# A second 7-product block in every other pair of MLP chunks, with splits in one piece

## The chip, the cores and the metric

The kernel runs on one core of one Trainium2 chip. The metric is the device time of one execution in microseconds. The kernel before takes 2026.78 us, the median of three runs (2024.16 to 2027.75). Five engines run their own queues of instructions in order: TensorE (PE in the profile; its weight loads are shown apart as PEld), VectorE (DVE), ScalarE (ACT), GpSimd (POOL) and SyncE (SP). The last two mostly issue transfers here.

## What is computed

Two layers of a decoder work on x, 256 tokens by 2048 values in float32. The first layer mixes tokens by latent attention and a pooling mixer, the second by a gated short convolution. Each is followed by the part that the change touches:

```
h = rmsnorm(x, mlp_norm_g[layer])
x = x + square(relu(h @ w_up)) @ w_down     # w_up 2048 x 8192, w_down 8192 x 2048
```

The result has float32 accuracy, which the kernel reaches by splitting: every matrix is taken as a high and a low part in the format fp32r, and a product is three matmuls, high by high, high by low, low by high.

## The kernel before

**Splitting the weights.** Weights come as slabs of 1 MB (128 partitions by four blocks of 512 columns) into one of three buffers, tag "raw", loaded through SyncE's queue. `halved` splits a slab in two pieces of 128x1024: ScalarE casts a piece to the high part (line 141), VectorE subtracts to get the low part (line 142). There are six buffers for high and six for low pieces, used in turn; a piece's cast cannot start before TensorE has done its last matmul on the piece six before.

**The MLP.** `mlp` takes the 8192 hidden columns in 16 chunks of 512, two by two: eight pairs. `up_chunk` multiplies h by four slabs of w_up (lines 161 and 162, through `columns_steps`, 16 pairs of matmuls a slab), adds the two halves of the sum (line 195 a copy by ScalarE, line 197 a sum by VectorE), takes relu (732) and square (734), splits the hidden values into hT (201, 202) and forms four differences of them (746 to 748), which are split into fT. The down product of a pair of chunks runs in the time of the next pair's up chunks.

**The 7-product form.** For the first seven pairs, columns 0 and 1 of the down product (two blocks of 512 of the 2048 columns) are made by `down_seven`: seen as 2 by 2 blocks on tokens and hidden rows, the product needs seven block products in place of eight (the form of Strassen and Winograd). A product is 12 matmuls of 512 columns (lines 772 to 774). Its right sides are weight blocks b11, b12, b21, b22 and sums of them. The sums are made by transfers that add into the buffers t and v in memory on chip, issued by GpSimd (line 766), four for each pair. Three products go straight onto x (`onto`, line 801, a VectorE instruction that scales by r2, the reciprocal mean square of each token, and adds); four go into the totals p1, p5, p6, p7 (line 794), which are combined onto x in the seventh pair. Columns 2 and 3 are made by `down_block`, 96 matmuls for both (lines 154 to 156), with sums onto x at line 864. The last pair has four such plain blocks and no up chunks beside it.

**What sets the order.** The program text gives only a list of steps: generators of the up chunks, the products and the plain blocks are advanced in an order written out in the loop over p. A scheduler then places every instruction in its engine's queue by when it takes it to be ready, so the order in a queue is not the order of the text. Once built, each queue is fixed: an instruction that waits holds up all behind it on its engine. On VectorE the splits, the sums of products and the work on hidden values share one queue.

Of the kernel before, what the change touches and what calls it, by code (L numbers as in the profile page):

```python
# [16 lines left out]
P = 128  # L17
# [50 lines left out]
def trunk(ctx: ExitStack, tc, x_in, pos_in, mix_g, mlp_g, w_up, w_down, w_in, qa_g, kva_g, w_uq, w_ukv,  # L68
# [8 lines left out]
    def new_stage(raw_bufs=0, **more):  # L77
# [11 lines left out]
    small = ctx.enter_context(tc.tile_pool(name="small", bufs=2))  # L89
    acts = ctx.enter_context(tc.tile_pool(name="acts", bufs=4))  # L90
# [32 lines left out]
    def slab(src, kt, cols, sub=2, dmas=1, pieces=None):  # L123
# [8 lines left out]
    def halved(raw, sub=2, pieces=None):  # L132

        kt, cols = raw.shape[1], raw.shape[2]
        out_ = []
# [42 lines left out]
    def columns_steps(pss, w, xT, c0, n):  # L178
# [3 lines left out]
        for s in range(KD // rows_):  # L182
            ws = slab(w[s * rows_ * P:(s + 1) * rows_ * P, c0:c0 + n * P], rows_, n * P, sub=rows_ // 2)
# [8 lines left out]
    def sum_halves(ps, name):  # L192

        t = small.tile([P, 2, S], F32, tag="t", name=uid("t"))
        nc.scalar.copy(t, ps[:, :, S:2 * S])  # L195
        u = small.tile([P, 2, S], F32, tag="u", name=uid(name))
        nc.vector.tensor_tensor(out=u, in0=ps[:, :, 0:S], in1=t, op=ALU.add)
        return u
# [15 lines left out]
    new_stage(3)  # L214
# [71 lines left out]
    def squares(ss, b):  # L286

        for t in range(T):
            junk = small.tile([P, NB], F32, tag="t", name=uid("junk"))
# [22 lines left out]
    def over_tokens(r, pool):  # L312

        ps = bank2()
        for t in range(T):
            rb = small.tile([P, P], F32, tag="rb", name=uid("rb"))
# [54 lines left out]
    def latents():  # L371
# [12 lines left out]
        for t in range(T):  # L384
            for i in range(2):
                junk = small.tile([P, NB], F32, tag="t", name=uid("junk"))
# [77 lines left out]
    for g in reversed(range(GROUPS)):  # L464
        ps = bank2()
        for s in range(2):
            c0 = LAT + g * 2 * P
            ws = slab(w_in[0, s * 8 * P:(s + 1) * 8 * P, c0:c0 + 2 * P], 8, 2 * P, sub=4)
# [20 lines left out]
        m = small.tile([P, 2, S], F32, tag="u", name=uid("pm"))  # L489
# [6 lines left out]
    def rotate(src, t, heads, tables):  # L496

        own, other = (a[:, t, :].unsqueeze(1).to_broadcast([P, heads, ROPE]) for a in tables)
        turned = small.tile([P, heads, ROPE], F32, tag="t", name=uid("turned"))
# [5 lines left out]
    def square_sum(out_, a):  # L505
        n = a.shape[1]
        junk = small.tile([P, NB], F32, tag="t", name=uid("junk"))
# [69 lines left out]
    ws = slab(pool_w[0].rearrange("g c d -> (g c) d"), 2 * GROUPS, 2 * P, sub=4)  # L577
# [134 lines left out]
    def mlp(layer, ss, xT, after=None):  # L712
        up, down = w_up[layer], w_down[layer]
        hid, sums, totals = {}, {}, {}
# [4 lines left out]
        def up_chunk(c):  # L719

            pss = []
            yield from columns_steps(pss, up, xT, c * NB, 4)
            hT = act_tile()
            seven = c < 2 * (pairs - 1)
            if seven:
                fT = pools["forms"].tile([P, 2, 2, 4, P], F32R, tag="fT", name=uid("fT"))
            hid[c] = hT
            if seven:
                sums[c] = fT
            for i, ps in enumerate(pss):  # L730
                u = sum_halves(ps, "h")
                nc.scalar.activation(u, u, AF.Relu)
                sq = small.tile([P, 2, S], F32, tag="sq", name=uid("sq"))
                nc.scalar.activation(sq, u, AF.Square)
                split(hT[:, 2 * i:2 * i + 2, 0:S], hT[:, 2 * i:2 * i + 2, S:2 * S], sq)
                if seven:
                    sum_forms(fT[:, i], sq.rearrange("p e (t s) -> p (e t) s", t=T))
# [5 lines left out]
        def sum_forms(fT, a):  # L743

            f = small.tile([P, 4, P], F32, tag="u", name=uid("f"))
# [5 lines left out]
        def down_seven(pair):  # L751
# [3 lines left out]
            rows_ = down[2 * pair * NB:2 * (pair + 1) * NB].rearrange("(q e p) n -> e p q n", e=2, p=P)  # L755

            def at(e, n):
                return rows_[e][:, :, n * NB:(n + 1) * NB]
# [9 lines left out]
            def product(o, b, left):  # L768

                for q, (hi, lo) in enumerate(halved(b)):  # L770
# [3 lines left out]
                    nc.tensor.matmul(o, lhsT=a_lo, rhs=hi, start=False, stop=q == 3)  # L774

# [9 lines left out]
            def summed(name, o):  # L785

                if pair == 0:
                    totals[name] = pools["forms"].tile([P, NB], F32, tag=name, name=uid(name), bufs=1)
                    nc.scalar.copy(totals[name], o)
                else:  # L790
                    plus(totals[name], totals[name], o)

            def plus(out_, a, b):
                nc.vector.tensor_tensor(out=out_, in0=a, in1=b, op=ALU.add)

            def minus(out_, a, b):
                nc.vector.tensor_tensor(out=out_, in0=a, in1=b, op=ALU.subtract)

            def onto(t, n, part):
                xb = x[:, t, n * NB:(n + 1) * NB]  # L800
                nc.vector.scalar_tensor_tensor(out=xb, in0=part, scalar=r2[0][:, t:t + 1], in1=xb, op0=ALU.mult, op1=ALU.add)

            yield
            b11 = block(0, 0)
            t = block(0, 1, "t")
            add(t, 0, 0)
            one = bank2()
            product(one[:, 0, :], b11, own(0, 0))
            summed("p1", one[:, 0, :])
            yield  # L810
            v = block(0, 1, "v")
            add(v, 1, 1)
            product(one[:, 1, :], t, form(1))
            add(t, 1, 1)
            summed("p5", one[:, 1, :])
            yield
            two = bank2()
# [164 lines left out]
```

## Time and profile before

| | before |
|---|---|
| runs, median of 3 | 2026.78 us (2024.16 to 2027.75) |
| the profiled execution | 2025.33 us |
| its span | 2023.5 us |
| TensorE busy | 2005.9 us, 99%, 10534 matmuls |
| VectorE busy | 1389.5 us, 69%, 1739 instructions |
| ScalarE busy | 1120.1 us, 55%, 1480 instructions |
| GpSimd busy | 124.4 us, 6% |
| read from memory | 453.79 MB, 225 GB/s over the span |

The span is the time between the first and the last instruction of the profiled execution; its own time has 1.8 us around it. "Busy" counts an instruction from its start to its end; on TensorE and VectorE one starts before the last has ended, so durations add to more than the time they take together. In rows of a timeline the first number is the start, the second the duration, and in brackets stands the idle time before, with what ended it. In a table by windows the second number is the window's length, and behind the five engines' busy times (with counts) come the granted clock of TensorE (1.00 is full speed), the share of the 16 DMA engines that was busy, and GB/s. Rows of grouped instructions give their count, busy time and mean duration (ns), and end with the idle time just before them and what ended it.

### The profile page before, as it was taken

Reading aid. Unit: us, or ns where it says so; the run is one execution under the profiler, and the core shown is the slowest. Engines: PE = TensorE matmul, PEld = TensorE weight load, DVE = VectorE, ACT = ScalarE, POOL = GpSimd, SP = SyncE. Lnnn points to the kernel's source line nnn. Section 1 sums busy time; section 2 is a strip of 40 time slices with the busy share of each in tenths; the row PEclk is TensorE's granted clock in tenths of the full one; section 3 lists DMA queues with packets and bytes.
Section 4 is the critical chain, followed back from the end, with each engine's and each line's share of the span. In section 5 each row is a group of like instructions: output and inputs, shape, how many; then the busy total and the mean of one; then the engine's idle time right before and its main releaser. Section 6 shows DMA issues by size and latency. Waiting matters only on the chain.

```text
span 2023.5 us, 26714 instructions
## 1 busy us (share of the span) xinstructions
PE 2005.9 (99%) x10534; PEld 1722.5 (85%) x10534; DVE 1389.5 (69%) x1739; ACT 1120.1 (55%) x1480; POOL 124.4 (6%) x132
## 2 busy tenths in 40 slices
PE   8999999999999999999999999999999999999999
PEld 7987888888888888888888888888888888888887
DVE  5767567677766777776666656567777777777774
ACT  5457456565555655555444444456555566555552
POOL 2240000000000000000000000000000000000000
PEclk9999999999999999999999999999999999999999
DMA  7555577998989889865555557758898988989773
GB/s 245 161 173 177 182 219 215 270 247 242 281 252 264 245 258 257 263 208 187 179 190 188 190 191 226 231 177 222 267 255 265 270 239 265 257 253 270 217 224 125
DMA packets 232782, 457.62 MB, mean 226 GB/s; under 512 B 7344, under 2 KB 17456, under 8 KB 232656
## 3 DMA queue, kind: packets, MB, share of 16 engines
q1 hardware_dynamic: 202704, 396.91, 58.5%
q0 software_dynamic: 29920, 59.00, 17.1%
q8 instruction: 82, 1.34, 0.3%
q14 instruction: 44, 0.36, 0.0%
q10 hardware_dynamic: 32, 0.01, 0.0%
HBM read 453.79 MB, written 2.10 MB: 225 GB/s over the span
## 4 chain that ended last, share of the span: by engine, by line
PE 98%; DMA 1%; ACT 1%; SPq 0%; issue 0%; DVE 0%; ACTq 0%
PE ps L161 32%; PE ps L162 16%; PE ps L154 11%; PE ps L155 11%; PE ps L156 11%; PE ps L772 4%; PE ps L774 4%; PE ps L773 4%; PE ps L167 1%; PE ps L168 1%; PE ps L169 1%; PE ps L298 1%; DMA raw<-in_even_w_in 1%; PE ps L615 0%; ACT hi L141 0%; PE ps L619 0%
## 5 line engine op out<-in xcount | busy, mean ns | idle before, releaser
L142 DVE TENSOR_TENSOR lo<-raw,hi 128x1024 fp32r<-128x1024 f32 (+2 forms) x694 | 847.8, 1227 | 413.9 <-ACT hi L141 409.6
L141 ACT CAST hi<-raw 128x1024 fp32r<-128x1024 f32 (+2 forms) x694 | 724.8, 1049 | 620.9 <-PE ps L161 285.2
L161 PE MATMUL ps<-xT,hi 128*128 128x512 f32 x2816 | 988.9, 394 | 0.0
L162 PE MATMUL ps<-xT,lo 128*128 128x256 f32 x2816 | 789.5, 280 | 0.0
L161 PEld LDWEIGHTS ps<-xT,hi 128*128 128x128 f32 x2816 | 529.5, 188 | 122.1
L162 PEld LDWEIGHTS ps<-xT,lo 128*128 128x128 f32 x2816 | 527.6, 187 | 3.7
L154 PE MATMUL ps<-hi,hT 128*128 128x512 f32 (+1 forms) x896 | 349.1, 390 | 0.0
L156 PE MATMUL ps<-hi,hT 128*128 128x512 f32 (+1 forms) x896 | 347.3, 388 | 0.0
L155 PE MATMUL ps<-lo,hT 128*128 128x512 f32 (+1 forms) x896 | 347.2, 388 | 0.0
L154 PEld LDWEIGHTS ps<-hi,hT 128*128 128x128 f32 x896 | 168.3, 188 | 35.1 <-issue 1.3
L156 PEld LDWEIGHTS ps<-hi,hT 128*128 128x128 f32 x896 | 168.2, 188 | 34.7
L155 PEld LDWEIGHTS ps<-lo,hT 128*128 128x128 f32 x896 | 168.3, 188 | 33.6 <-DVE lo L142 0.4
L142 DVE TENSOR_TENSOR lo<-t,hi 128x1024 fp32r<-128x1024 f32 x84 | 102.6, 1221 | 45.2 <-ACT hi L141 45.1
L141 ACT CAST hi<-t 128x1024 fp32r<-128x1024 f32 x84 | 87.3, 1051 | 73.2 <-PE ps L161 50.7
L766 POOL DMA_DIRECT2D t<-in_w_mlp_down x42 | 54.4, 1296 | 1107.0 <-DVE lo L142 720.3
L772 PE MATMUL ps<-hi,fT 128*128 128x512 f32 x224 | 88.1, 393 | 0.0
L774 PE MATMUL ps<-hi,fT 128*128 128x512 f32 x224 | 87.7, 391 | 0.0
L773 PE MATMUL ps<-lo,fT 128*128 128x512 f32 x224 | 87.1, 389 | 0.0
L195 ACT COPY t<-ps 128x512 f32<-128x512 f32 x88 | 50.9, 579 | 40.6 <-PE ps L162 40.4
L772 PE MATMUL ps<-hi,hT 128*128 128x512 f32 x168 | 65.8, 392 | 0.0
L774 PE MATMUL ps<-hi,hT 128*128 128x512 f32 x168 | 65.6, 391 | 0.0
L773 PE MATMUL ps<-lo,hT 128*128 128x512 f32 x168 | 65.4, 389 | 0.0
(186 smaller groups left out, 1582.3 us busy)
## 6 DMA issues: line engine op xcount, KB each, us to landing
raw<-in_w_mlp_up SPq DMA_DIRECT2D x128, 1024.0 KB, 7.2
raw<-in_w_mlp_down SPq DMA_DIRECT2D x114, 1024.0 KB, 6.4
raw<-in_odd_w_in SPq DMA_DIRECT2D x48, 1024.0 KB, 5.1
t<-in_w_mlp_down POOLq DMA_DIRECT2D x42, 1024.0 KB, 13.5
raw<-in_even_w_out SPq DMA_DIRECT2D x16, 1024.0 KB, 5.4
raw<-in_odd_w_out SPq DMA_DIRECT2D x16, 1024.0 KB, 5.3
t<-in_w_mlp_down SPq DMA_DIRECT2D x14, 1024.0 KB, 5.8
v<-in_w_mlp_down SPq DMA_DIRECT2D x14, 1024.0 KB, 5.8
```

The costliest lines, as they stand in the source:

```text
L141: a = nc.scalar.copy(h, r)
L142: v = nc.vector.tensor_tensor(out=l, in0=r, in1=h.bitcast(F32), op=ALU.subtract)
L154: nc.tensor.matmul(o, lhsT=a_hi, rhs=hi[:, c0:c0 + n], start=first, stop=False)
L155: nc.tensor.matmul(o, lhsT=a_hi, rhs=lo[:, c0:c0 + n], start=False, stop=False)
L156: nc.tensor.matmul(o, lhsT=a_lo, rhs=hi[:, c0:c0 + n], start=False, stop=last)
L161: nc.tensor.matmul(o, lhsT=hi[:, c0:c0 + P], rhs=act[:, kt, :], start=first, stop=False)
L162: nc.tensor.matmul(o[:, S:2 * S], lhsT=lo[:, c0:c0 + P], rhs=act[:, kt, 0:S], start=False, stop=last)
L195: nc.scalar.copy(t, ps[:, :, S:2 * S])
L766: nc.gpsimd.dma_start(b, at(e, n), accum_op=ALU.add)
L772: nc.tensor.matmul(o, lhsT=a_hi, rhs=hi, start=q == 0, stop=False)
L773: nc.tensor.matmul(o, lhsT=a_hi, rhs=lo, start=False, stop=False)
L774: nc.tensor.matmul(o, lhsT=a_lo, rhs=hi, start=False, stop=q == 3)
```

## The change

Three things are changed.

First, a slab is split in one piece of 128x2048, with three buffers for high and three for low parts of that size (the same memory as six of half the size). The first stage alone, with the attention's latent columns, keeps six, in which some slabs are smaller.

Second, in the first, third, fifth and seventh pair (p even, "double") columns 2 and 3 take the 7-product form as well. Its steps are named with a prime, one' to four'. Here the sums of weight blocks are made by VectorE (`combine`, four of 128x2048 each), not by transfers, and the products go straight onto x, with r2 or its negative, except two that go into one total "w", which is combined onto x in the seventh pair. Such a pair loads ten weight blocks for the down product where it loaded nine (five and four). The forms of chunk A are made at the end of the chunk. The second, fourth and sixth pair keep the plain blocks.

Third, the order of steps is written as a list of names, and small buffers share one tag of four. Lines move: the split is 143 and 144 in the changed kernel (141 and 142 before), the up matmuls 163 and 164 (161, 162), a product 783 to 785 (772 to 774), sums into totals and weight blocks 798 (794), sums onto x 810 (801).

```diff
-    def slab(src, kt, cols, sub=2, dmas=1, pieces=None):
+    def slab(src, kt, cols, sub=None, dmas=1, pieces=None):
...
+        sub = sub or kt
...
-        for wanted in (dict(raws=raw_bufs, halves=6) if raw_bufs else {}, more):
+        for wanted in (dict(raws=raw_bufs, halves=half_bufs) if raw_bufs else {}, more):
...
     def sum_halves(ps, name):
 
-        t = small.tile([P, 2, S], F32, tag="t", name=uid("t"))
-        nc.scalar.copy(t, ps[:, :, S:2 * S])
-        u = small.tile([P, 2, S], F32, tag="u", name=uid(name))
-        nc.vector.tensor_tensor(out=u, in0=ps[:, :, 0:S], in1=t, op=ALU.add)
+        u = small.tile([P, 2, S], F32, name=uid(name), **T4)
+        nc.scalar.copy(u, ps[:, :, S:2 * S])
+        nc.vector.tensor_tensor(out=u, in0=ps[:, :, 0:S], in1=u, op=ALU.add)
         return u
...
+            def combine(out_, a, b, op):
+                nc.vector.tensor_tensor(out=out_, in0=a, in1=b, op=op)
+
+            def onto(t, n, part, r=0):
+                xb = x[:, t, (n0 + n) * NB:(n0 + n + 1) * NB]
+                nc.vector.scalar_tensor_tensor(out=xb, in0=part, scalar=r2[r][:, t:t + 1], in1=xb, op0=ALU.mult, op1=ALU.add)
...
+            def one():
+                b11 = block(0, 0)
+                w["v"] = block(0, 1, "v")
+                p = product(b11, own(0, 0))
+                combine(w["v"], w["v"], b11, ALU.add)
+                onto(0, 0, p)
+                summed("w", p)
+
+            def five():
+                p = product(w["v"], form(1))
+                onto(0, 1, p)
+                onto(1, 1, p)
+
+            def three():
+                w["t"] = block(0, 1, "t")
+                b22 = block(1, 1)
+                p = product(b22, form(3))
+                combine(w["t"], w["t"], b22, ALU.add)
+                combine(w["v"], w["v"], b22, ALU.add)
+                onto(0, 1, p)
+
+            def seven():
+                p = product(w["t"], form(0))
+                onto(1, 1, p)
+                onto(1, 0, p, 1)
+
+            def six():
+                summed("w", product(w["v"], form(2)), ALU.subtract)
+
+            def two():
+                b21 = block(1, 0)
+                p = product(b21, own(0, 1))
+                combine(w["v"], w["v"], b21, ALU.add)
+                onto(0, 0, p)
+
+            def four():
+                onto(1, 0, product(w["v"], own(1, 1)))
+                if final:
+                    onto(0, 1, totals["w"], 1)
+                    onto(1, 0, totals["w"])
+                    onto(1, 1, totals["w"], 1)
...
+        ONE_SEVEN = ("one A five A three A seven A six n A A n A two B four B B B m B B m B", "A one A five three A seven A six n A A n A two B four B B B m B B m B")
+        TWO_SEVENS = "one A five A three A seven A six one' A A two B five' B four B three' seven' six' A B two' B B four' B"
         for p in range(pairs - 1):
-            products = down_seven(p)
...
+            double = p % 2 == 0
+            steps = dict(A=up_chunk(2 * p + 2, double), B=up_chunk(2 * p + 3), n=down_block(p, 2, False), m=down_block(p, 3, False))
+            products = down_seven(p, 0, False)
+            if double:
+                products.update((k + "'", f) for k, f in down_seven(p, 2, True).items())
+            for step in (TWO_SEVENS if double else ONE_SEVEN[p > 0]).split():
+                if step in products:
+                    products.pop(step)()
+                else:
+                    next(steps[step], None)
```

In the order's rows a name's number tells its buffers apart; "hi" and "lo" are the parts of a slab, "raw", "t" and "v" weight blocks, "ps" a product on TensorE's side, "h" a chunk's hidden values.

The middle of the third pair of the first layer, on VectorE, before: splits of the buffer t for "six" (lo799, lo801), of the block for "two" (lo805, lo807) and of an up slab (lo820, lo822), in halves.

```order
L142 TENSOR_TENSOR lo799_4826<-t754_4559,hi798_4825 128x1024
L142 TENSOR_TENSOR lo801_4830<-t754_4559,hi800_4829 128x1024
L142 TENSOR_TENSOR lo805_4851<-raw803_4848,hi804_4850 128x1024
L794 TENSOR_TENSOR p7544_3357<-p7544_3357,ps777_4695 128x512
L142 TENSOR_TENSOR lo807_4855<-raw803_4848,hi806_4854 128x1024
L142 TENSOR_TENSOR lo820_4917<-raw818_4914,hi819_4916 128x1024
L197 TENSOR_TENSOR h811_4886<-ps760_4584,t810_4884 128x512
L142 TENSOR_TENSOR lo822_4921<-raw818_4914,hi821_4920 128x1024
```

The same place now; the up slab is lo628, "six" is lo612, one' is lo617, and "two" is lo623:

```order
L144 TENSOR_TENSOR lo612_4473<-t584_4239,hi611_4472 128x2048
L144 TENSOR_TENSOR lo617_4496<-raw613_4490,hi616_4495 128x2048
L198 TENSOR_TENSOR h619_4515<-ps587_4259,h619_4515 128x512
L144 TENSOR_TENSOR lo623_4532<-raw621_4529,hi622_4531 128x2048
L798 TENSOR_TENSOR p6450_3221<-p6450_3221,ps605_4416 128x512
L198 TENSOR_TENSOR h620_4522<-ps588_4260,h620_4522 128x512
L144 TENSOR_TENSOR lo628_4553<-raw626_4550,hi627_4552 128x2048
```

Between the splits of the block for "two" and of the up slab stand a sum into p6 and a sum of hidden values. On TensorE, at that place now, the last matmuls on the up slab before "two", and the first of "two" (hi622 and lo623):

```order
L164 MATMUL ps625_4549<-xT326_2237,lo628_4553 128x256
L163 MATMUL ps624_4548<-xT326_2237,hi627_4552 128x512
L164 MATMUL ps624_4548<-xT326_2237,lo628_4553 128x256
L163 MATMUL ps624_4548<-xT326_2237,hi627_4552 128x512
L783 MATMUL ps615_4494<-hi622_4531,hT541_3895 128x512
L784 MATMUL ps615_4494<-lo623_4532,hT541_3895 128x512
```

Eleven matmuls of the up slab stand before "two", and the other 21 behind it.

The end of the same pair on VectorE, before: lo837 and lo839 are splits of t for "four", ps797 is "two", ps835 is "four".

```order
L142 TENSOR_TENSOR lo837_5019<-t754_4559,hi836_5018 128x1024
L864 SCALAR_TENSOR_TENSOR x_79<-ps802_4847,r2468_2923,x_79 128x512 x2
L142 TENSOR_TENSOR lo839_5023<-t754_4559,hi838_5022 128x1024
L142 TENSOR_TENSOR lo842_5042<-raw840_5039,hi841_5041 128x1024
L801 SCALAR_TENSOR_TENSOR x_79<-ps797_4824,r2468_2923,x_79 128x512
L142 TENSOR_TENSOR lo844_5046<-raw840_5039,hi843_5045 128x1024
```

The same place now: ps647 is two', lo667 the split of v for four', ps665 four', lo672 the next up slab. On TensorE two', four' and that slab follow one another.

```order
L810 SCALAR_TENSOR_TENSOR x_79<-ps647_4742,r2392_2775,x_79 128x512
L144 TENSOR_TENSOR lo667_4861<-v614_4492,hi666_4860 128x2048
L203 TENSOR_TENSOR fT650_4760<-f652_4767,fT650_4760 128x512
L203 TENSOR_TENSOR hT659_4831<-h660_4832,hT659_4831 128x2x256
L751 TENSOR_TENSOR f662_4840<-h660_4832 128x256
L203 TENSOR_TENSOR hT659_4831<-h663_4846,hT659_4831 128x2x256
L752 TENSOR_TENSOR f662_4840<-h660_4832,f662_4840 128x128
L753 TENSOR_TENSOR f662_4840<-h660_4832,f662_4840 128x128
L810 SCALAR_TENSOR_TENSOR x_79<-ps665_4859,r2392_2775,x_79 128x512
L144 TENSOR_TENSOR lo672_4882<-raw670_4879,hi671_4881 128x2048
```

The sum of the product before stood behind the split for the last product; it now stands ahead of it, and the sum of the last product ahead of the next slab's split.

The end of the seventh pair, on VectorE now: ps965 in the sum is three', lo969 the split for seven', lo972 for six'. Ahead of these rows stand the eight instructions that combine p1, p5, p6 and p7 onto x.

```order
L144 TENSOR_TENSOR lo967_7247<-raw964_7243,hi966_7246 128x2048
L798 TENSOR_TENSOR t963_7241<-t963_7241,raw964_7243 128x2048
L810 SCALAR_TENSOR_TENSOR x_79<-ps965_7245,r2392_2775,x_79 128x512
L144 TENSOR_TENSOR lo969_7266<-t963_7241,hi968_7265 128x2048
L144 TENSOR_TENSOR lo972_7285<-v937_7025,hi971_7284 128x2048
L144 TENSOR_TENSOR lo975_7304<-raw973_7301,hi974_7303 128x2048
```

The sum of three' stands between the splits for three' and seven'; before, this pair had the splits of plain blocks there.

More of the change, by code (lines that the diff above doesn't have):

```diff
@@ L717, in mlp, with up_chunk @@
         pairs = DFF // NB // 2
-        def up_chunk(c):
-            pss = []
+        def up_chunk(c, late=False):
+            pss, kept = [], []
             yield from columns_steps(pss, up, xT, c * NB, 4)
[L723 to L729, printed above, removed]
+            hT = hid[c] = act_tile()
             for i, ps in enumerate(pss):
@@ L803, in down_seven @@
[L803 to L817, printed above, removed]
-            product(two[:, 0, :], block(1, 1), form(3))
@@ L819, in down_seven @@
-            onto(0, 1, two[:, 0, :])
-            yield
-            product(two[:, 1, :], v, form(0))
-            summed("p7", two[:, 1, :])
-            yield
-            three = bank2()
-            product(three[:, 0, :], t, form(2))
-            add(t, 1, 0)
-            summed("p6", three[:, 0, :])
-            yield
-            product(three[:, 1, :], block(1, 0), own(0, 1))
-            onto(0, 0, three[:, 1, :])
-            yield
-            four = bank2()
-            product(four[:, 0, :], t, own(1, 1))
@@ L834, in down_seven @@
[L834 to L843 removed]
+                    combine(totals[name], totals[name], o, op)
@@ new lines, in three @@
+            def three():
+                onto(0, 1, product(block(1, 1), form(3)))
+            def seven():
+                summed("p7", product(w["v"], form(0)))
+            def six():
+                p = product(w["t"], form(2))
+                add(w["t"], 1, 0)
+                summed("p6", p)
+            def two():
+                onto(0, 0, product(block(1, 0), own(0, 1)))
+            def four():
+                onto(1, 0, product(w["t"], own(1, 1)))
+                if final:
+                    p1, p5, p6, p7 = (totals[k] for k in ("p1", "p5", "p6", "p7"))
+                    onto(0, 0, p1)
+                    combine(p1, p1, p6, ALU.subtract)
+                    combine(p6, p5, p1, ALU.subtract)
+                    onto(0, 1, p6)
+                    combine(p1, p1, p7, ALU.subtract)
+                    onto(1, 0, p1)
+                    combine(p5, p5, p1, ALU.subtract)
+                    onto(1, 1, p5)
@@ new lines, in down_seven, with one, five @@
+            if not own_sums:
+                return dict(one=one, five=five, three=three, seven=seven, six=six, two=two, four=four)
+            def one():
+                b11 = block(0, 0)
+                w["v"] = block(0, 1, "v")
+                p = product(b11, own(0, 0))
+                combine(w["v"], w["v"], b11, ALU.add)
+                onto(0, 0, p)
+                summed("w", p)
+            def five():
+                p = product(w["v"], form(1))
+                onto(0, 1, p)
+                onto(1, 1, p)
```

114 lines of the change are left out of this document (59 added, 55 removed).

## The prediction, before the changed kernel was run

> **What bounds the kernel now.** I read the page first, then the chain of waits, then the two 88 us windows of the first MLP, then single instructions on TensorE (PE) and VectorE (DVE). The page and its chain:
>
> ```profile
> span 2023.5 us, 26714 instructions
> PE 2005.9 (99%) x10534; PEld 1722.5 (85%) x10534; DVE 1389.5 (69%) x1739; ACT 1120.1 (55%) x1480; POOL 124.4 (6%) x132
> ...
> q1 hardware_dynamic: 202704, 396.91, 58.5%
> q0 software_dynamic: 29920, 59.00, 17.1%
> ...
> PE 98%; DMA 1%; ACT 1%; SPq 0%; issue 0%; DVE 0%; ACTq 0%
> ```
>
> The chain is TensorE's own work from end to end. Inside the first MLP it is busy without a gap at clock 1.00, while VectorE has about a quarter of the time free and the transfers a tenth:
>
> ```profile
> core 0: us, PE busy (x) PEld busy (x) DVE busy (x) ACT busy (x) POOL busy (x), PEclk, DMA share, GB/s
> 323.00:411.00 88.00, 88.00 (x450) 74.61 (x449) 64.89 (x79) 57.19 (x73) 5.11 (x4) 1.00 0.89 251
> 411.00:499.00 88.00, 88.00 (x448) 74.86 (x447) 65.14 (x78) 51.78 (x60) 5.13 (x4) 1.00 0.91 261
> ```
>
> The waits show why there is slack: VectorE waits for ScalarE's cast, the cast waits until TensorE gives a buffer back, and behind the splits TensorE's weight loads of one plain line waited 0.4 us for a split in the whole run.
>
> ```profile
> DVE lo L142 <- ACT hi L141: 489.0, 428, 6.1
> ...
> ACT hi L141 <- PE ps L161: 360.0, 222, 1.8
> ```
> ```profile
> L155 PEld LDWEIGHTS ps<-lo,hT 128*128 128x128 f32 x896 | 168.3, 188 | 33.6 <-DVE lo L142 0.4
> ```
>
> So a matmul removed is worth its full time as long as the splits stay ahead, and whether they do is the whole question.
>
> **What the change removes.** A product of the 7-product form is 12 matmuls of 512 columns. TensorE's timeline gives their pace:
>
> ```profile
> 425.67 0.39 PE L161 MATMUL ps<-xT,hi 128*128 128x512 f32 x1
> ...
> 426.02 0.39 PE L161 MATMUL ps<-xT,hi 128*128 128x512 f32 x1
> ...
> 427.77 0.39 PE L772 MATMUL ps<-hi,fT 128*128 128x512 f32 x1
> ...
> 430.51 0.40 PE L161 MATMUL ps<-xT,hi 128*128 128x512 f32 x1
> ```
>
> From 427.77 to 430.51 one product takes 2.74 us, 0.228 us a matmul. An up slab is 16 pairs of L161 and L162 at 0.35 us (425.67 to 426.02), 5.6 us. A pair of up chunks is now 8 up slabs, 7 products and 96 plain matmuls: 44.8 + 19.2 + 21.9 = 85.9 us. In a pair where columns 2 and 3 change form ("double" from here), 84 matmuls stand for the 96, so it is 83.1 us. The saving is 2.74 us for each of 8 double pairs, **21.9 us**, if TensorE never waits.
>
> **What it adds on VectorE.** The rows behind the costs:
>
> ```profile
> 411.68 1.40 DVE L864 SCALAR_TENSOR_TENSOR x<-ps,r,x 128x512 f32<-128x512 f32 x2
> 413.00 1.21 DVE L142 TENSOR_TENSOR lo<-t,hi 128x1024 fp32r<-128x1024 f32 x1
> 414.13 1.22 DVE L142 TENSOR_TENSOR lo<-raw,hi 128x1024 fp32r<-128x1024 f32 x1
> 415.26 0.68 DVE L794 TENSOR_TENSOR p<-p,ps 128x512 f32<-128x512 f32 x1
> 415.86 1.22 DVE L142 TENSOR_TENSOR lo<-raw,hi 128x1024 fp32r<-128x1024 f32 x1
> ```
> ```profile
> L142 DVE TENSOR_TENSOR lo<-raw,hi 128x1024 fp32r<-128x1024 f32 x676 | 827.1, 1229 | 399.9 <-ACT hi L141 395.6 <-PE ps L162 2.7
> L141 ACT CAST hi<-raw 128x1024 fp32r<-128x1024 f32 x676 | 707.3, 1050 | 609.5 <-PE ps L161 285.2 <-PE ps L156 102.1 <-DMA raw<-in_w_mlp_down 60.6
> L141 ACT CAST hi<-raw 128x1088 fp32r<-128x1088 f32 x15 | 16.2, 1099 | 10.6 <-DMA raw<-in_even_w_in 6.8 <-PE ps L156 3.7
> L195 ACT COPY t<-ps 128x512 f32<-128x512 f32 x88 | 50.9, 579 | 40.6 <-PE ps L162 40.4
> L197 DVE TENSOR_TENSOR h<-ps,t 128x512 f32<-128x512 f32 x64 | 43.9, 687 | 11.2 <-ACT t L195 11.1
> L801 DVE SCALAR_TENSOR_TENSOR x<-ps,r,x 128x512 f32<-128x512 f32 x42 | 31.3, 746 | 0.0
> ```
>
> Queued behind each other, VectorE's steps follow after 1.13 us (1024 columns), 0.60 us (512, L794) and 0.66 us (512, onto x). No row has a 128x2048 step. From 0.688 us at 512 (L197) and 1.229 at 1024 the slope is 0.541 per 512, so 2048 should take 1.229 + 2 x 0.541 = 2.31 us, or 2.19 after the step before it; the lower bound is by the start-to-start times, 1.22 + 2 x 0.53 = 2.28, the upper twice the duration, 2.46. For the cast, 0.579 at 512 (L195, a copy) and 1.050 at 1024 give 1.99 at 2048; 1.050 and the 1.099 of a 1088-column cast give 1.050 + 16 x 0.049 = 1.83. I take 1.91, the middle. That half as many instructions do the splits is worth almost nothing in bulk (2.19 against 2 x 1.13).
>
> A double pair's VectorE work: 22 splits (19 now) and 4 sums of weight blocks at 2.19 are 57.0; 17 sums of products (7 + 10) and 12 sums and splits of the hidden values at 0.60 are 17.4; forms, about 4. That is **78 of 83.1 us, 94%**, against some 74% in the windows above. It still fits, so the mean does not decide; the order of the queue does.
>
> **Transfers.** Queue q1 moved 396.91 MB in 58.5% of 2023.5 us, so a 1 MB block takes 3.13 us of the engines, and an accumulating one (59.00 MB in 17.1%) 6.15. A double has one load more on SyncE's queue, 18, and the same 4 accumulations on GpSimd's: 56.3 + 24.6 = 80.9 of 83.1 us, 97%, against 17 loads, 77.8 of 85.9, now. I put no wait on this: q1's loads can be issued three buffers early, and TensorE's new waits would lengthen the pair. Uncovered it costs one load, 3.13 us, per double.
>
> **Where TensorE comes to wait.** With three 128x2048 buffers a slab's cast cannot begin before TensorE has left the slab three before. Cast and split in a row are 1.91 + 2.31 = 4.2 us, against two products, 5.5 us: 1.3 us to spare, and every sum in VectorE's queue that must wait for a product to end, and stands ahead of the next split, uses it up. Four kinds of place, in the changed kernel's order, whose rows for A, B, C and D the part on the change quotes (line 144 is the split there, 810 the sum onto x, 783 to 785 a product):
>
> (A) Middle of the third and the seventh pair. TensorE takes eleven matmuls of an up slab (split lo628) before "two" (lo623), and VectorE splits lo623 first. From the start of "six": the copy 0.58, cast to 2.5, split lo623 to 4.8, two sums to 6.0, split lo628 to 8.3. TensorE is through six, one' and two high-part matmuls at 5.9. The wait is 2.4, at the least 1.1 (lo628 right behind its cast, which can start when six is over: 2.74 + 1.91 + 2.31 = 7.0). I take 2.3, near the upper end, because the rows in between stand in a fixed queue.
>
> (B) End of the same pairs. The sum of two' onto x stands directly ahead of the split for four', which is TensorE's next product: 0.66 + 2.31 + about 0.1 of hand-off, less 0.23 for the one matmul that needs no low part, is 2.8.
>
> (C) Behind four' of the third pair the sum stands ahead of the next up slab's split: three matmuls can run, so 0.66 + 2.31 + 0.1 - 0.69 = 2.4.
>
> (D) Seventh pair, three' to seven': a sum of three' stands ahead of seven's split, two matmuls can run: 2.6.
>
> The first pair adds about 2.5 and the fifth 3.8 (an up slab between seven' and six', the ends), and the last down blocks 1.5 behind the seventh pair; here several small covers add up, and zero is possible. Per layer: 2.5 + (2.3 + 2.8 + 2.4) + 3.8 + (2.3 + 2.6 + 2.8 + 1.5) = 23. The second, fourth and sixth pair I cost at nothing: there the sums of weight blocks are absent, VectorE has its present spare time, and if that cover failed, each would cost a wait of B's size, 2.8.
>
> Elsewhere only one place feels the longer piece: the first pool columns behind the latents, where TensorE waits 1.94 us for a cast now (row under rival 3) and that cast grows by 1.91 - 1.05 = 0.9.
>
> Sum: 2025.3 (the profiled execution, 1.5 under the median) - 21.9 + 2 x 23 + 0.9 = **2050 us**. Lower end of this case: A at 1.1 and the small ones at zero, 2 x 12.8 = 26 of waits, 2030. Upper: the eight sums that combine the totals in the seventh pair (about 5 us, ahead of three's split) and a third more on the rest, 60 of waits, 2064.
>
> **Rivals.** Break-even is 2.74 us of waits per double pair; my sum has 5.8.
>
> (1) The cover holds. The order before has the same kind of disorder (in the middle of its third pair too), and TensorE lost nothing. Then 2025.3 - 21.9 = 2003. Against it: then six half-size buffers let VectorE run on in pieces of 1.13 us, and at the end of that pair the split for "four" stood ahead of the sum of "two", where now it stands behind.
>
> (2) A part of the waits, 18 to 26 us, cancels the gain: 2021 to 2030.
>
> (3) The waits also cost clock. The trace has two waits of this size:
>
> ```profile
> 67.70 0.39 PE L167 MATMUL ps<-xT,hi 128*128 128x256 f32 x1 [1.94 <-ACT hi L141]
> ```
> ```profile
> 60.00:68.00 8.00, 6.06 (x38) 5.80 (x37) 1.02 (x6) 4.18 (x8) 0.00 (x0) 1.00 0.00 0
> 68.00:72.00 4.00, 4.00 (x36) 4.00 (x35) 3.09 (x5) 4.00 (x12) 0.00 (x0) 1.00 0.18 21
> ```
> ```profile
> 158.72 0.39 PE L167 MATMUL ps<-hT,hi 128*128 128x256 f32 x1 [3.01 <-ACT qkv L522]
> ```
> ```profile
> 155.00:160.00 5.00, 1.61 (x10) 1.20 (x10) 4.65 (x13) 4.94 (x14) 1.12 (x1) 0.92 0.81 271
> 160.00:162.00 2.00, 2.00 (x11) 2.00 (x11) 0.67 (x2) 1.52 (x10) 0.00 (x0) 0.50 0.95 370
> 162.00:164.00 2.00, 2.00 (x17) 2.00 (x17) 1.02 (x4) 1.39 (x8) 0.00 (x0) 0.84 0.00 0
> ```
>
> The 3.01 us wait is followed by a granted clock of 0.50: 5 x 0.08 + 2 x 0.50 + 2 x 0.16 = 1.7 us lost; around the 1.94 us one it stays at 1.00, before and after. My waits of 2.3 to 2.8 lie between. If all twelve of them cost the clock: 12 x 1.7 = 21, 2071. For the forecast I take no loss, since each stays below 3.01. [...]
>
> (4) One load per double comes late: 8 x 3.13 = 25 on the forecast, 2075. For it, 97%; against it, the windows above at 0.89 and 0.91 show no gap.
>
> **How the numbers follow.** Forecast (2030 to 2064) 0.54; cover holds (2003, up to 2014) 0.18; cancelled 0.10; clock 0.13; loads 0.05. About 0.2%, 4 us, can be told from no change (2022.7 to 2030.8 around the median). Faster takes the cover case and 0.04 of the cancelled: 0.22. Same takes 0.05 of the cancelled and 0.02 from the forecast's foot: 0.07. Slower, 0.71. The range reaches down into the cover case and up into those of clock and loads: 2006 to 2074; the forecast's own is 2030 to 2064.
>
> **What would show it.** 96 matmuls fewer on TensorE; splits of 128x2048 near 2.3 us and casts near 1.9; in the third and seventh pairs idle time of TensorE before low-part matmuls and before four', released by VectorE, 2 to 3 us a time; double pairs of 83 plus 2.5 to 9 us, others at 85.9; VectorE's share near 90% in the doubles. Wrong would be: double pairs of 83 us without gaps (the cover holds), gaps that ScalarE or a transfer releases, gaps in the second, fourth and sixth pairs, or granted clocks under 0.9 behind the gaps.

## The result, and the profile after

The changed kernel takes 2120.91 us, the median of four runs (2119.75 to 2128.13), against 2025.86 us for the kernel before: a ratio of 1.0475, 95% interval 1.0461 to 1.0489. It is 95 us slower. The forecast had the sign and put the loss at 25 us.

The page of the changed kernel (its profiled execution took 2128.13 us, the longest of the four):

```profile
span 2126.3 us, 25410 instructions
PE 2031.2 (96%) x10438; PEld 1718.4 (81%) x10438; DVE 1499.2 (71%) x1455; ACT 1101.4 (52%) x1112; POOL 124.4 (6%) x132
...
PE 68%; DMA 12%; DVE 11%; ACT 5%; issue 3%; POOL 1%; SPq 0%; DVEq 0%; ACTq 0%; POOLq 0%
```

TensorE has 96 matmuls fewer and yet is busy 25 us longer; idle is 2126.3 - 2031.2 = 95.1 us, against 17.6. The chain of waits, 98% TensorE before, now runs through transfers, VectorE and ScalarE for more than a quarter of the span.

Where in the program: by the starts of the first down product of each layer and of the norm behind the first MLP, the first MLP takes 713.0 us (669.5 before), the stretch between the two MLPs' products 384.9 (381.7), the second MLP to the end 698.7 (647.2). Windows of the first MLP, from one double pair's start to the next (a double and the plain pair behind it, and the seventh alone), of the changed kernel; below them one pair of the kernel before:

```profile
core 0: us, PE busy (x) PEld busy (x) DVE busy (x) ACT busy (x) POOL busy (x), PEclk, DMA share, GB/s
329.70:511.30 181.60, 174.16 (x863) 144.20 (x862) 139.83 (x122) 106.08 (x95) 10.26 (x8) 0.99 0.87 249
511.30:698.30 187.00, 174.67 (x861) 145.20 (x860) 140.31 (x122) 99.35 (x81) 10.32 (x8) 0.98 0.84 242
698.30:877.40 179.10, 172.62 (x862) 144.35 (x861) 139.79 (x122) 99.75 (x81) 10.29 (x8) 0.99 0.89 252
877.40:972.00 94.60, 85.02 (x426) 70.33 (x424) 79.58 (x66) 49.85 (x39) 2.77 (x4) 1.00 0.63 189
```
```profile
411.10:496.75 85.65, 85.65 (x437) 72.89 (x436) 62.79 (x75) 50.04 (x58) 5.13 (x4) 1.00 0.91 260
```

Without waits the seven pairs would take 4 x 82.9 + 3 x 85.65 = 588.6 us; they take 642.3. So the layer loses 54 us, of which 642.3 - 606.5 = 36 us are idle time of TensorE (the forecast had 23) and the rest lower clock and the cost of starting again, below. VectorE's work in a double is 139.8 - 62.8 = 77 us, as computed (78). The DMA share falls below the old 0.91, to 0.63 in the seventh pair: the DMA engines are not full on the average, so their rate alone does not explain a late load.

The added steps cost what was computed for each alone (line, engine, forms, count, then busy us and mean ns):

```profile
L144 DVE TENSOR_TENSOR lo<-raw,hi 128x2048 fp32r<-128x2048 f32 x330 | 755.5, 2291 | 314.9 <-ACT hi L143 314.3
L143 ACT CAST hi<-raw 128x2048 fp32r<-128x2048 f32 x330 | 628.9, 1909 | 488.1 <-PE ps L163 228.8 <-PE ps L785 85.4 <-issue 67.6
...
L798 DVE TENSOR_TENSOR v<-v,raw 128x2048 f32<-128x2048 f32 x24 | 54.9, 2290 | 47.8 <-DMA v<-in_w_mlp_down 26.4 <-DMA raw<-in_w_mlp_down 21.4
```

2.29 and 1.91 us, against estimates of 2.31 and 1.91. The last row shows what the forecast left out: VectorE stood still 47.8 us ahead of sums of weight blocks, 26.4 us of it for the load of v itself and 21.4 us for the raw block to be added.

**What a wait costs.** TensorE in the changed kernel, first pair, around a wait for a split:

```profile
397.14 0.39 PE L783 MATMUL ps<-hi,fT 128*128 128x512 f32 x1
398.50 0.50 PE L784 MATMUL ps<-lo,fT 128*128 128x512 f32 x1 [0.97 <-DVE lo L144]
...
401.17 0.39 PE L783 MATMUL ps<-hi,fT 128*128 128x512 f32 x1
```

The product takes 401.17 - 397.14 = 4.03 us in place of 2.74. It loses 1.29 us, 0.32 more than the idle time shown. The shown idle time leaves out that the matmul before the gap lasts 0.39 us where its neighbours follow after 0.23, and that the one behind the gap takes 0.50 us. And the clock, around two waits of the second pair:

```profile
476.91 0.50 PE L783 MATMUL ps<-hi,hT 128*128 128x512 f32 x1 [0.93 <-ACT hi L143]
479.24 0.50 PE L784 MATMUL ps<-lo,hT 128*128 128x512 f32 x1 [1.83 <-DVE lo L144]
```
```profile
477.00:480.00 3.00, 1.17 (x4) 0.77 (x5) 3.00 (x3) 3.00 (x2) 0.00 (x0) 0.99 0.34 126
480.00:483.50 3.50, 3.50 (x10) 2.69 (x9) 3.50 (x2) 0.46 (x1) 0.00 (x0) 0.52 0.77 214
```

Neither gap alone comes near the 3.01 us of the kernel before, and still the granted clock falls to 0.52 for the next 3.5 us. Single gaps of nearly one size do not agree either. In the third pair, behind a gap of 2.90 us that ended at 567.07 the clock stays at 1.00 (also from 567.00 to 569.00); behind one of 2.74 us that ended at 601.64 it falls to 0.60:

```profile
569.00:583.00 14.00, 14.00 (x76) 11.99 (x75) 11.05 (x11) 5.11 (x3) 0.00 (x0) 1.00 0.81 253
```
```profile
602.00:606.00 4.00, 4.00 (x13) 3.04 (x11) 2.43 (x7) 4.00 (x3) 0.00 (x0) 0.60 0.89 287
```

So in this trace the length of one gap does not tell whether the clock falls. The mean granted clock of the execution is 0.986 (0.998 before); by estimate that is (0.998 - 0.986) x 2126 = 26 us. So the 102.8 us between the two profiled spans are: -21.9 for the matmuls, +77.5 of idle time, +26 of clock, and some 21 left. If each of some 60 gaps in the MLPs costs 0.32 us more than it shows, as the one above, that is 19 of them.

**Two waits that were not foreseen.** In the third pair, VectorE, then the waits of TensorE that follow (the rows are of two engines):

```profile
557.57 0.75 DVE L810 SCALAR_TENSOR_TENSOR x<-ps,r,x 128x512 f32<-128x512 f32 x1
562.52 2.29 DVE L798 TENSOR_TENSOR v<-v,raw 128x2048 f32<-128x2048 f32 x1 [4.19 <-DMA raw<-in_w_mlp_down]
564.73 2.28 DVE L144 TENSOR_TENSOR lo<-raw,hi 128x2048 fp32r<-128x2048 f32 x1
```
```profile
567.07 0.38 PE L164 MATMUL ps<-xT,lo 128*128 128x256 f32 x1 [2.90 <-DVE lo L144]
```

The sum of b21 into v stands ahead of an up slab's split and waits 4.19 us for its block, whose load was issued at 552.99. TensorE pays 2.90 us for it. And in the second pair, a plain one, ScalarE's cast of t waits for an accumulating transfer (GpSimd issues it behind another that waits for the load of v):

```profile
453.84 1.28 POOL L773 DMA_DIRECT2D v<-in_w_mlp_down  x1 [21.56 <-DMA v<-in_w_mlp_down]
454.59 1.85 POOL L773 DMA_DIRECT2D t<-in_w_mlp_down  x1
```
```profile
474.96 1.90 ACT L143 CAST hi<-t 128x2048 fp32r<-128x2048 f32 x1 [7.09 <-DMA t<-in_w_mlp_down]
```

These are the two waits of 0.93 and 1.83 us above. Such pairs were costed at nothing.

### The profile page after: what moved, and what is told of

The parts are those of the page before. It is cut to its first block, busy times and chain, and to the rows that moved or that the text cites. A ratio compares the mean times of both kernels' runs of the same rounds, so it can differ in the third digit from the quotient of the medians.

```text
span 2126.3 us, 25410 instructions
## 1 busy us (share of the span) xinstructions
PE 2031.2 (96%) x10438; PEld 1718.4 (81%) x10438; DVE 1499.2 (71%) x1455; ACT 1101.4 (52%) x1112; POOL 124.4 (6%) x132
## 4 chain that ended last, share of the span: by engine, by line
PE 68%; DMA 12%; DVE 11%; ACT 5%; issue 3%; POOL 1%; SPq 0%; DVEq 0%; ACTq 0%; POOLq 0%
PE ps L163 24%; PE ps L164 13%; DVE lo L144 8%; PE ps L157 6%; PE ps L156 6%; PE ps L158 6%; DMA t<-in_w_mlp_down 5%; ACT hi L143 4%; PE ps L784 4%; PE ps L785 3%; PE ps L783 3%; DMA raw<-in_w_mlp_down 3%; DMA v<-in_w_mlp_down 2%; DMA raw<-in_w_mlp_up 1%; DVE x L810 1%
## 5 line engine op out<-in xcount | busy, mean ns | idle before, releaser
L144 DVE TENSOR_TENSOR lo<-raw,hi 128x2048 fp32r<-128x2048 f32 (+2 forms) x348 | 776.1, 2233 | 331.5 <-ACT hi L143 331.0
L143 ACT CAST hi<-raw 128x2048 fp32r<-128x2048 f32 (+2 forms) x348 | 646.3, 1862 | 501.0 <-PE ps L163 228.8
L157 PE MATMUL ps<-lo,hT 128*128 128x512 f32 (+1 forms) x640 | 248.1, 388 | 4.2 <-DVE lo L144 4.2
L156 PE MATMUL ps<-hi,hT 128*128 128x512 f32 (+1 forms) x640 | 249.5, 390 | 0.9 <-DVE rT L611 0.9
L158 PE MATMUL ps<-hi,hT 128*128 128x512 f32 (+1 forms) x640 | 247.7, 387 | 0.0
L143 ACT CAST hi<-t 128x2048 fp32r<-128x2048 f32 x50 | 95.6, 1912 | 160.2 <-PE ps L163 64.0
L144 DVE TENSOR_TENSOR lo<-t,hi 128x2048 fp32r<-128x2048 f32 x50 | 114.4, 2288 | 59.7 <-ACT hi L143 59.6
L783 PE MATMUL ps<-hi,fT 128*128 128x512 f32 x352 | 140.1, 398 | 6.7 <-ACT hi L143 4.8
L156 PEld LDWEIGHTS ps<-hi,hT 128*128 128x128 f32 x640 | 120.2, 188 | 26.3 <-issue 1.3
L158 PEld LDWEIGHTS ps<-hi,hT 128*128 128x128 f32 x640 | 120.2, 188 | 24.4
L785 PE MATMUL ps<-hi,fT 128*128 128x512 f32 x352 | 137.8, 393 | 0.0
L783 PE MATMUL ps<-hi,hT 128*128 128x512 f32 x264 | 108.4, 412 | 11.4 <-ACT hi L143 6.5
L785 PE MATMUL ps<-hi,hT 128*128 128x512 f32 x264 | 107.6, 407 | 0.5 <-DVE hT L203 0.5
L144 DVE TENSOR_TENSOR lo<-v,hi 128x2048 fp32r<-128x2048 f32 x38 | 86.9, 2287 | 26.4 <-ACT hi L143 26.1
```

The costliest lines, as they stand in the source:

```text
L143: a = nc.scalar.copy(h, r)
L144: v = nc.vector.tensor_tensor(out=l, in0=r, in1=h.bitcast(F32), op=ALU.subtract)
L156: nc.tensor.matmul(o, lhsT=a_hi, rhs=hi[:, c0:c0 + n], start=first, stop=False)
L157: nc.tensor.matmul(o, lhsT=a_hi, rhs=lo[:, c0:c0 + n], start=False, stop=False)
L158: nc.tensor.matmul(o, lhsT=a_lo, rhs=hi[:, c0:c0 + n], start=False, stop=last)
L783: nc.tensor.matmul(o, lhsT=a_hi, rhs=hi, start=q == 0, stop=False)
```

## The experiments

All times stand beside the kernel before, which took 2025.7 to 2027.1 us each time that it was timed next to them.

**First: the parts one by one.** The change is undone along two lines, the pieces and the doubles.

The pieces back to two, doubles kept:

```diff
-        sub = sub or kt
+        sub = sub or max(1, kt // 2)
...
-    def new_stage(raw_bufs=0, half_bufs=3, **more):
+    def new_stage(raw_bufs=0, half_bufs=6, **more):
```

> The changed kernel, but every slab split in two pieces with six buffers for high and six for low pieces, as before the change; the double pairs and their order stay. Theory (a VectorE sum that waits for a product stands ahead of a split of one long piece): TensorE can start when the first half is split, so each wait of 2 to 3 us shrinks by about 1.1 us, and the lower clock behind the waits goes with them: 28 waits a layer, so some 30 to 60 us faster than the 2121 us of the change, 2060 to 2090. Rival (the double pairs' sums of weight blocks and their transfers are the cause, whatever the pieces): within 15 us of 2121.

2085.62 us, within the theory's range. But only the waits shrank (TensorE is idle 2083.1 - 2020.5 = 62.6 us, against 95.1): the granted clock, which was to recover with them, stays at 0.985. The doubles undone, pieces kept:

```diff
-            double = p % 2 == 0
+            double = False
```

> The changed kernel with no double pair (columns 2 and 3 plain in every pair), splits still in one piece with three buffers. Theory (long pieces hurt only where waiting sums crowd VectorE's queue): up to 10 us over the kernel before, 2026 to 2036. Rival (the long pieces with three buffers are bad everywhere): 2050 or more.

2052.49 us, on the side of the rival. Both undone:

> The changed kernel with no double pair and with splits in two pieces and six buffers: what is left is the shared small buffers and the list of steps. Both theories: the time of the kernel before, 2026 within 4 us. A longer time would mean that the small changes cost something.

2033.29 us (2031.42 to 2037.97; ratio 1.0033, 1.0013 to 1.0052): 7 us more than before and outside the 4 us that were allowed, so the small changes were not free. The four make a table:

| | two pieces, six buffers | one piece, three buffers |
|---|---|---|
| no doubles | 2033.3 | 2052.5 |
| doubles | 2085.6 | 2120.9 |

The long pieces cost 19 us without doubles and 35 with them. The doubles cost 52 with half pieces and 68 with long ones; as they save 21.9 us of matmuls, they make 74 and 90 us of waits and lower clock. The theory put the loss on one thing, long pieces behind waiting sums; but the doubles lose without long pieces too, and the long pieces lose without doubles. That loss is thin and spread out: between the profiled spans without doubles, 2049.1 and 2036.2, 5.6 us of the 12.9 lie in the first MLP, 5.5 in the second and 1.7 ahead of them, and TensorE's recorded waits for low parts of up slabs are twelve of at most 1.1 us.

What of the 7 us? The change has one part more, which its description leaves out: the products take the banks of PSUM, the memory for TensorE's results, from one list for the whole MLP, so the first product of a pair can share a buffer with the last of the pair before. Before, each pair began with a new one. One more edit on that form gives each pair a list of its own:

```diff
-            w = {}
+            w, banks = {}, []
```

> The kernel with neither doubles nor long pieces (2033 us), with one more edit: a pair's seven products take PSUM banks of their own and no longer put the first product of a pair into the free half of the bank in which the last product of the pair before still waits to be summed. Theory (that sharing makes TensorE wait for VectorE's sum, 5.1 us of idle in six waits there, and some more for the restarts): back to the kernel before, 2026 to 2028. Rival (the shared small buffers cost it): 2032 or more.

2029.51 us, ratio 1.0007 (0.9998 to 1.0016): not to be told from the kernel before, if a little over the theory's 2028. The six waits for a sum (5.1 us) are gone. The same edit with doubles and half pieces:

> Doubles with splits in two pieces (2086 us), and banks of their own for each group of seven products. Theory: the waits of TensorE for a sum onto x (23.6 us of idle before products in that run) go, with their restarts and lower clock: 2045 to 2065. Rival (they are VectorE's lateness, which shows elsewhere then): 2075 or more.

2099.62 us, 14 us slower than without the edit. This expectation failed: the waits moved to the plain blocks' sums (28.0 us of idle of TensorE before products behind line 920, in six waits of up to 6.2 us). So in the doubles the wait went from one bank to another. That VectorE's lateness is behind both fits, but the edit also leaves half of a two-bank buffer unused in each group of seven, and the two were not separated.

**Second: the order of the sums.** The prediction's waits B, C and D came from a sum that stands ahead of a split. Here each sum of a product of the 7-product form is made only behind the split that comes next in the text (the sums of weight blocks and of the plain blocks keep their place):

```diff
+    def run_later():
+        todo = later[:]
+        later.clear()
+        with behind(*last_prep):
+            for f in todo:
+                f()
...
+        run_later()
         return out_
...
             def onto(t, n, part, r=0):
+                later.append(lambda: onto_now(t, n, part, r))
```

> The changed kernel with one edit in VectorE's order: a sum of a product onto x or into a total may only stand behind the split of the next slab. Theory: the waits at the end of the third and seventh pair and behind them (B, C, D of the prediction, 2.6 to 2.8 us idle each, about 0.3 more for the restart) go, some 20 us for the two layers, and with them some lower clock: 2085 to 2105. Rival (VectorE is simply too full in the double pairs): the wait moves to another split, 2115 or more.

2116.32 us, only 4.6 us faster: the rival. The place B shows why. VectorE in the changed kernel at the end of the third pair (line 798 adds b21 into v, 144 is the split for four', 810 the sum of two'), and TensorE's wait for it:

```profile
594.07 2.28 DVE L798 TENSOR_TENSOR v<-v,raw 128x2048 f32<-128x2048 f32 x1
...
598.63 0.75 DVE L810 SCALAR_TENSOR_TENSOR x<-ps,r,x 128x512 f32<-128x512 f32 x1 [0.68 <-PE ps L785]
599.30 2.28 DVE L144 TENSOR_TENSOR lo<-v,hi 128x2048 fp32r<-128x2048 f32 x1
```
```profile
601.64 0.50 PE L784 MATMUL ps<-lo,hT 128*128 128x512 f32 x1 [2.74 <-DVE lo L144]
```

With the sum behind (line 807 adds b21, 152 is the split, 825 the sum):

```profile
592.87 2.29 DVE L807 TENSOR_TENSOR v<-v,raw 128x2048 f32<-128x2048 f32 x1
...
597.19 2.29 DVE L152 TENSOR_TENSOR lo<-v,hi 128x2048 fp32r<-128x2048 f32 x1 [0.64 <-ACT hi L151]
...
600.00 0.75 DVE L825 SCALAR_TENSOR_TENSOR x<-ps,r,x 128x512 f32<-128x512 f32 x1
```
```profile
599.54 0.50 PE L793 MATMUL ps<-lo,hT 128*128 128x512 f32 x1 [1.83 <-DVE lo L152]
```

The order is as wanted and the wait falls from 2.74 to 1.83 us, no more. The split was late whatever stood ahead: VectorE sums b21 into v, ScalarE casts, VectorE splits, 2.29 + 1.92 + 2.29 = 6.5 us in a row, and in the changed kernel VectorE had come to that sum without a pause from 584.62 on. The sum of two' was the last 0.9 us of a longer lateness. What else stands in that row, the sum of b21 ahead of the split, was not moved, so this run tells of the sums of products alone.

**Third: VectorE's sums of weight blocks.** They can cost by their work, or by their waits for loads and by the time that they keep a raw buffer. Work cut, waits kept (a raw block is still held until the sum, which is now some 2 us shorter):

```diff
-                combine(w["v"], w["v"], b11, ALU.add)
+                combine(w["v"][:, :, 0:1], w["v"][:, :, 0:1], b11[:, :, 0:1], ALU.add)
```

(the other three alike)

> The changed kernel, with VectorE's four sums of weight blocks per double pair cut to one column of each block of 512 (so the result is not the reference's: the rest of the sum is left out). The waits for the loads and the hold on the raw buffers stay; 8 x 4 x 2.2 = 70 us of VectorE's work go, and the scheduler's order moves a little. Theory 1 (VectorE at 94% in the double pairs is what makes TensorE wait): 30 to 60 us faster than 2121, 2060 to 2090. Theory 2 (late loads: a raw block stays in its buffer until VectorE has summed it, and VectorE stands still for loads): 2105 or more.

2061.51 us, 59 us faster. Work kept, the waits for a raw block and the holds gone, with every engine's order as it was (the waits for v and t themselves stay, 33.4 us of VectorE's idle time in that run):

```diff
-                combine(w["v"], w["v"], b11, ALU.add)
+                combine(w["v"], w["v"], w["v"], ALU.add)
```

> The changed kernel, with each of VectorE's four sums of weight blocks adding the buffer to itself (the other block is left out of the sum, so the result is not the reference's). VectorE's work and all engines' orders stay; gone are the sums' waits for a raw block and its longer hold on one of three raw buffers. Theory 2 (late loads): 20 to 40 us faster than 2121, 2080 to 2100. Theory 1 (VectorE's work): 2110 or more.

2101.16 us (2095.36 and 2106.97), 14 to 26 us faster. The middle, 2101, lies between the ranges of the two theories; the two runs had a granted clock of 0.994 and 0.988, which is about what parts them. So both theories hold in part, and the work weighs more. The cut of the first edit took 32 sums from 2.29 to 0.17 us, 65 us of VectorE's busy time, and gave 59. Not all of the 59 is waiting: the mean granted clock is 0.998, as before the change, against 0.988 and 0.989 in the middle runs of the changed kernel, which is by estimate 0.0095 x 2121 = 20 us. The other 39 are shorter waits and fewer of them. TensorE's waits for splits are

```profile
PE ps L164 <- DVE lo L144: 20.3, 17, 1.8
PE ps L784 <- DVE lo L144: 7.7, 6, 1.3
```

(total, times, longest us); in the changed kernel they were

```profile
PE ps L164 <- DVE lo L144: 29.7, 20, 3.3
...
PE ps L784 <- DVE lo L144: 23.1, 13, 2.8
```

Is it the amount, or the place of one of the sums? The last of the four alone cut (in the chain at the end of the pair), and the first alone, the same edit at one place each:

> The changed kernel with only the last of the four sums of weight blocks (b21 into v, ahead of four') cut to one column of each block of 512 (the rest of that sum is left out). By amount: a quarter of the 59 us that all four cost, about 15, so 2106. By place (sum 2.3, cast 1.9 and split 2.3 in a row against 5.5 us of two products, at the end of each double pair): half of the 59 or more, 2085 to 2095.

> The changed kernel with only the first of the four sums (b11 into v, between one' and five') cut to one column of each block of 512 (the rest of that sum is left out). By amount: about 2106, as for the last sum. By place (here a whole up slab and more lies between the sum and the product that needs it): 2112 or more.

2094.97 us and 2102.91 us: 26 and 18 us faster. The last costs nearly half of the 59, as by place (2085 to 2095); the first, to which the theory of place gave at most 9, costs 18, somewhat more than a quarter, as by amount. So both count; how much each carries was not separated, and the two sums in the middle were not cut alone.

Sums moved to GpSimd, which is busy 6% of the time:

```diff
-                combine(w["v"], w["v"], b11, ALU.add)
+                nc.gpsimd.tensor_tensor(out=w["v"], in0=w["v"], in1=b11, op=ALU.add)
```

> The changed kernel with the four sums of weight blocks per double pair on GpSimd in place of VectorE, nothing left out. Theory 1 (VectorE's work): faster than 2121 by 20 us or more, if GpSimd's sum of 128x2048 takes less than some 5 us, which no run has shown. Theory 2 (late loads): no gain or a loss, since the sums hold the raw buffers as long or longer, and GpSimd's queue, which also issues the accumulating transfers, stands still for the loads: 2115 to 2160.

> The same with splits in two pieces and six buffers (beside the 2086 us of that form with VectorE's sums). Theory 1: 2040 to 2070. Theory 2: 2080 or more.

2136.79 us, and 2113.65 with half pieces: slower than with the sums on VectorE by 16 and 28. This did not relieve VectorE, whose busy time rose from 1499.2 to 1525.0 us with 32 sums fewer, so it tells nothing against the theory of work. The timelines of GpSimd and of VectorE in the first:

```profile
411.52 5.12 POOL L889 TENSOR_TENSOR v<-v,raw 128x2048 f32<-128x2048 f32 x1
```
```profile
411.54 5.66 DVE L203 TENSOR_TENSOR fT<-f,fT 128x512 fp32r<-128x512 f32 x1 [0.41 <-ACT fT L202]
...
417.58 0.68 DVE L798 TENSOR_TENSOR w<-w,ps 128x512 f32<-128x512 f32 x1
```

GpSimd's sum takes 5.12 us, and a VectorE subtraction of 128x512 that starts 0.02 us behind it takes 5.66 us where the same form takes 0.68 in the changed kernel: it ends at 417.20, 0.56 us behind the end of GpSimd's sum.

**Fourth: how many doubles.** In the first and fifth pair only, and, with half pieces and banks of their own, in the fifth alone (the totals are combined in the last double then):

```diff
-            double = p % 2 == 0
+            double = p % 4 == 0
```

> The changed kernel with doubles in the first and the fifth pair only (the third and seventh plain). By the changed kernel's trace a double and the pair behind it lose 12.6 us (first), 18.0 (third), 10.1 (fifth) and 11.5 (seventh, alone) against 82.9 and 85.6 us. If the loss belongs to each double by itself, the third and the seventh take 2 x (18.0 - 2.7 + 11.5 - 2.7) = 48 us with them and plain pairs in one piece cost some 8 back: about 2080. If one double only hands its lateness on to the next, more goes: 2060 or less.

> Splits in two pieces, banks of their own, and a double in the fifth pair alone, the mildest one. Theory (a double costs VectorE and the loads more than TensorE gains, even alone): 2030 to 2040, over the kernel without doubles of the same form. Rival (one double, with plain pairs around it, keeps its 2.7 us): two doubles, 5 us faster than the same form without, 2021 to 2023, and faster than the kernel before.

2086.83 us: near the 2080 of a loss that belongs to each double by itself. And 2045.88 us (ratio 1.0093, 1.0071 to 1.0114), against 2029.5 for the same form with none: 16 us for two doubles, more than was expected. The mildest double, alone among plain pairs, ends 8 us behind a plain pair; with the 2.7 us that it saves it loses some 11.

**Fifth: are the 96 matmuls ever won?** Half pieces and the four sums cut:

> Doubles with splits in two pieces and six buffers (2086 us), all four sums of weight blocks cut to one column of each block of 512 (the rest is left out). If the 96 matmuls that the change saves are won once VectorE has room: 2033 (the same form without doubles) - 22 = 2011, up to 2025 with what waits are left. If the doubles lose by their loads and the ten sums of products as well: 2035 or more.

2042.20 us. No: with 63 us of VectorE's work gone and half pieces the doubles still take 9 us more than none (2033.3). TensorE is idle 37.1 us there, against 22.5 without doubles, and the clock was 0.992 to 0.994 against 0.997 or 0.998, which is some 6 to 12 us of 2042. ScalarE's casts waited 74.0 us for accumulating transfers into t, up to 11.8 us at a time; in the kernel before and in the one without doubles no such wait is on record (for raw blocks of w_down they waited 50.9 us here, 60.6 and 53.8 there). Whether these transfers alone take the rest, or VectorE's ten sums of products as well, was not separated.

## Why the prediction was right and wrong

- **The saving, 21.9 us.** Right as a term: 96 matmuls fewer, and an undisturbed product keeps its 2.74 us.
- **Durations.** Right: 2.29 us for the split and the sum, 1.91 for the cast, 77 us of VectorE's work in a double, 93% of the 82.9 us that TensorE would need without waits.
- **"It still fits, so the mean does not decide; the order of the queue does."** This is the step that failed. The waits were costed place by place, as if VectorE were on time at each and only the instructions just ahead of a split counted. Putting the sums of products behind the splits gave 4.6 us back; cutting VectorE's sums of weight blocks gave 59 (39 of waits, 20 of clock) for 65 us of work, and even the first sum alone, with a whole up slab between it and its product, gave 18. At this load, with the splits bound to three buffers and to loads, VectorE does not make good what it loses.
- **A to D.** The waits are where they were said to be: idle times of 2.06 and 1.65 (A, 2.3 predicted), 2.74 and 2.79 (B, 2.8), 1.64 and 0.18 (C, 2.4), 1.31 and 1.33 (D, 2.6 predicted as one) in the first layer. Their sizes fit, their cause only in part: B hardly depends on the sum that stands ahead. And they are 13.7 of the 36 us of idle time in the seven pairs; the other 22 lie where the sum had 2.5, 3.8 and 1.5 us or nothing.
- **Transfers: "I put no wait on this."** Wrong. The DMA engines had time left (a share of 0.63 to 0.89 in the pairs). VectorE waited 47.8 us for loads ahead of its sums into v, and a raw block now stays until VectorE has summed it: SyncE's loads into raw buffers waited 48.3 us for VectorE's sums into v, in eight waits, and 35.0 us for those into t, in four, where before none waited for such a sum. The waits for raw blocks and the holds are 14 to 26 us by the run with sums of a buffer with itself; what the waits for v and t cost was not measured. The rival's 25 us, one load per double, has that size, by luck: it counted bytes, not holds.
- **Plain pairs at nothing.** Wrong: the second, fourth and sixth pair have idle times of 2.8, 2.1 and 3.1 us in the first layer, the first and the last from a cast that waited over 7 us for an accumulating transfer. Gaps in these pairs, and gaps that a transfer releases, were among the prediction's own signs of being wrong.
- **The hand-off of 0.1 us.** Right: at B the split ends at 601.58 and the matmul starts at 601.64. What the sum lacks is the start again, about 0.3 us for each wait beyond its idle time (0.32 at the wait taken apart above).
- **The clock.** The forecast took no loss and a rival 21 us; it was 26 by the mean granted clock, on top of 77.5 us of added idle time where the forecast had 47. The prediction's reason, that each wait stays below 3.01 us, does not hold: two gaps of 0.93 and 1.83 us close together were enough (a clock of 0.52 behind them), and so was a single one of 2.74 (0.60), while one of 2.90 was not (1.00). What sets it was not shown.
- **The cover holds (2003).** Fell: even with VectorE's sums cut and half pieces the saving is not won.

## What to carry to other kernels

Here TensorE was the bound and VectorE fed it; before matmuls are taken away there by giving VectorE work, look whether VectorE has room for it. Its work came to 93% of TensorE's time in the changed pairs, and some 65 us of that work cut gave 59 us back with long pieces and 43 with half ones (part of it clock); the one reordering that was tried, of the sums of products, gave 5. A wait of TensorE cost its idle time plus some 0.3 us (0.32 where it was taken apart), plus a share for the clock, which by estimate was 26 us on 77.5 of added idle time. A block that a second engine had to read before its buffer was free held up the loads behind it (83.3 us of SyncE's waits, and 14 to 26 us of the kernel's time with the waits for the block), so count the hold and not only the bytes.

## What was not expected of the hardware

A VectorE instruction of 0.68 us took 5.66 us beside a GpSimd sum of 5.12 us and ended 0.56 us behind it. The granted clock fell to 0.52 after idle times of 0.93 and 1.83 us within 3.3 us, and to 0.60 after a single one of 2.74 us, all of them below the 3.01 us that the kernel before had shown; after one of 2.90 us it stayed at 1.00.
